# The order of small and big experts in a mixture-of-experts layer

## The chip, the cores and the metric

The kernel runs on one core of a Trainium2 chip. The metric is the device time of one execution in microseconds (us). TensorE does the matrix products, VectorE, ScalarE and GpSimd the elementwise work, SyncE (SP) issues nearly all transfers from device memory (HBM) into the on-chip memory. Each engine runs its own list of instructions in order; semaphores make one wait for another.

## The reference, cut to what matters

A two-layer transformer on 256 tokens of width 1,024, all in 32-bit floats: latent attention and a dense feed-forward layer, then a sparse attention and a mixture-of-experts layer (MoE). The change touches the MoE layer alone. There each token picks two of eight experts, and each expert has three matrices of 1,024 by 3,584 numbers:

```python
logits = (xt @ w_router)                     # 256 x 8
top_val, top_idx = lax.top_k(logits, 2)
wts = softmax(top_val)
for each expert e, on the tokens that picked it:
    h = silu(xb @ w_gate[e]) * (xb @ w_up[e])
    y[tokens] += (h @ w_down[e]) * weight
x = layer_norm(alpha * x + y)
```

The order in which the experts are taken does not enter the result, except through the rounding of the sum. An expert's matrices are 3 x 14 MB = 42 MB (1 MB is 1,024 KB in this text), all eight 336 MB, and each byte is read once.

## The kernel before, in words

**Positions.** The experts are worked off at eight positions. Position 0 is always expert 0, because its loads start before the router has decided. The others are put in order at run time: `arrange` ranks the experts by how many tokens picked them (rank 0 is expert 0, rank 1 the fullest of the rest, rank 7 the emptiest), and the constant `turn` says which rank stands at which position. SP reads the resulting expert numbers into registers and takes the addresses of its loads from them.

**Small and big.** A position in `PLAIN` (called small here) has 64 token slots. Its products take the 32-bit weights as they were loaded, as TensorE's moving operand, with the 64 slots in two halves of the array, and so need no preparation. A position outside `PLAIN` (big) has 128 slots. There each loaded half chunk is split into a rounded part and the rest (`split_half`: ScalarE copies into `whi`, VectorE subtracts into `wlo`), and each product is made of three (high by high, high by low, low by high). The splits go into a ring of half chunks `whi1` to `whi4` and `wlo1` to `wlo4`, so two whole chunks can be split ahead of TensorE. If more tokens picked an expert than it has slots (`most`), an extra pass runs at the end under a condition.

**Chunks and places.** Weights come in chunks of 1 MB, or 768 KB where a step is 1,536 columns wide. An expert has two steps (2,048 and 1,536 hidden columns; position 0 has three: 512, 2,048 and 1,024). For each step `run` does the gate products, half of the down products of the step before, the up products, the other half of the down products. The down products of an expert's last step thus fall between the gate and up products of the next expert. The loads follow this order exactly (`moe_keys`), one list of 364 chunks; position 1 starts with chunk 38, position 2 with chunk 82, position 7 with chunk 312.

Each chunk gets a place by `seq`, which always takes the place used longest ago. There are five raw buffers, seven tiles of 1 MB that are idle in this layer (`xTh`, `xTl`, `xna`, `lng`, `s2`, `x3Tl`, and `x3Th` from chunk 46 on), and the ring's five pairs `R0` to `R4`. The pairs `R1` to `R4` serve as places only up to the chunk in `until`, since the splits need them then; `R0` stays a place. After that there are 13 places, 12 once `lng` has been given back for the final norm's gain (at chunk 312). SP issues the loads in order; a load waits until its place is free: for a small expert when TensorE has used the chunk, for a big one when VectorE has made its `wlo`. A load that waits holds up all loads behind it.

**Order of the work.** TensorE's, VectorE's and ScalarE's order is written out by hand. `pump` splits the next half chunk after each chunk of products, at most five chunks ahead in the list. The MoE layer's first loads are issued from 381 us on, its first small products start at about 502 us.

The functions that the change touches and their surroundings:

Of the kernel before, what the change touches and what calls it, by code (L numbers as in the profile page):

```python
# [20 lines left out]
E = 8  # L21
FE = 3584
FF = 2816
PLAIN = 0, 1, 3, 5, 7


def body(tc, a, out, tap=None, upto=9):
# [31 lines left out]
    HL, NR = 5, 5  # L59
# [292 lines left out]
    if len(cols) % 2:  # L352
        c = plan[-1]
# [15 lines left out]
    def is_plain(key):  # L369

        return key[1] in PLAIN and key[:3] != ("mg", 0, 0)

# [29 lines left out]
    def moe_keys():  # L402
        prev = None
        for e in range(E):
            for j, (c0, wd) in enumerate(widths(e)):
                m = widths(prev[0])[prev[1]][1] // 256 if prev else 0
                for k, ds in (("mg", range((m + 1) // 2)), ("mu", range((m + 1) // 2, m))):
                    yield from ((k, e, j, i) for i in range(n_gu(wd)))
                    yield from (("md", *prev, i) for i in ds)
                prev = e, j  # L410
        yield from (("md", *prev, i) for i in range(wd // 256 - 2))
        yield from (("md", *prev, i, "tail") for i in range(2))
# [5 lines left out]
    keys = list(moe_keys())  # L418

    def seq():  # L420

        at = {f"raw{i}": n for i, n in enumerate((2, 3, 5, 6, 7))}
        at.update({z: first.index(z) for z in ("xTh", "xTl", "xna", "lng", "s2", "x3Tl")})
        at.update({i: first.index(R[i]) for i in range(HL)})

        at["x3Th"] = keys.index(("md", 0, 2, 0))

        until = dict.fromkeys(range(1, HL), keys.index(("mg", 2, 0, 0)) - 8)

        until["lng"] = keys.index(("mg", E - 1, 0, 0))  # L430
        yield from first
        n = len(first)
        while True:
            z = min((z for z in at if n < until.get(z, 9999)), key=at.get)
            at[z] = n
            n += 1
            yield R[z] if z in range(HL) else "raw" if z[:3] == "raw" else z

    seq = [z for _, z in zip(range(len(keys) + 2), seq())]
    for n, key in enumerate(keys):  # L440
        where = seq[n]
# [15 lines left out]
    tie, turn, most = off["tie"], off["turn"], off["most"]  # L457
# [1047 lines left out]
    def gather(e, base, gen=False):  # L1505

        G = {"plain": e in PLAIN and not gen}

# [348 lines left out]
    with tc.If(over > 0):  # L1857
        for e in range(E):
            count = nc.values_load(ordi[0:1, e:e + 1], min_val=0, max_val=256)
            for base in (64, 192) if e in PLAIN else (128,):  # L1860
                with tc.If(count > base):
# [19 lines left out]
def constants():  # L1881
    import numpy as np
    c = {}
    i = np.arange(128)
    c["ident"] = np.eye(128)
    c["tri"] = np.concatenate([np.zeros((128, 128)), np.where(i[None, :] > i[:, None], NEG, 0.0)], 1)
    c["utri"] = (i[:, None] < i[None, :]).astype(np.float64)
    c["iota"] = np.tile(np.arange(320.0), (128, 1))
    e = np.arange(8)
    c["jlt"] = np.tile((e[None, :] < e[:, None]).astype(np.float64).reshape(1, 64), (128, 1))  # L1890
    n = np.arange(16)
    cm = [((128 * t + i[:, None]) >= 16 * n[None, :] + 31) & (n[None, :] < 15) for t in range(2)]
    c["cmask"] = np.concatenate(cm, 1)
    freq = np.power(np.float32(10000.0), -np.arange(32, dtype=np.float32) / np.float32(32))
    ang = np.arange(256, dtype=np.float32)[:, None] * freq[None, :]
    lay = lambda z: np.concatenate([z[:128], z[128:]], 1)
    c["cos"], c["sin"] = lay(np.cos(ang)), lay(np.sin(ang))
    c["nsin"] = -c["sin"]
    c["tie"] = np.tile(np.where(e == 0, 1e6, -e.astype(np.float64)), (128, 1))
    c["turn"] = np.tile(np.array([0.0, 7, 1, 6, 2, 5, 3, 4]), (128, 1))  # L1900
    c["most"] = np.tile(np.where(np.isin(e, PLAIN), 64.0, 128.0), (128, 1))
    packed = np.concatenate([c[k].astype(np.float32) for k, _ in CONST_COLS], 1)
    assert packed.shape[1] == sum(n for _, n in CONST_COLS)
    idx = np.arange(384)
    dist = 255 - idx
    nn = np.maximum(dist, 0)
    nf = np.maximum(nn, 1).astype(np.float32)
    large = 16 + (np.log(nf / np.float32(16)) / np.float32(math.log(8.0)) * np.float32(16)).astype(np.int32)
    bk = np.where(nn < 16, nn, np.minimum(large, 31))
    oh = np.zeros((33, 384), np.float32)  # L1910
    oh[np.where(dist < 0, 32, bk), 383 - idx] = 1.0
    return {"consts": np.ascontiguousarray(packed), "bucket": oh}
# [26 lines left out]
```

## Time and profile before

| what | us |
|---|---|
| median of 3 runs (1328.12 to 1332.17) | 1328.43 |
| the profiled execution | 1331.11 |
| its span, first to last instruction | 1329.3 |

Shares of the span: TensorE 97%, its weight loads 69%, VectorE 54%, ScalarE 45%, GpSimd 2%; the transfers moved 429.52 MB (here millions of bytes), on average 323 GB/s over the span. The profiled execution is 1.8 us longer than its span, and 2.7 us over the median. A TensorE that is busy in the page is not TensorE at its peak, and a wait of it inside a group of products can hide in the busy time, so stretches are compared here by their length, and the loads by when they land.

### The profile page before, as it was taken

Reading aid. Unit: us, or ns where it says so; the run is one execution under the profiler, and the core shown is the slowest. Engines: PE = TensorE matmul, PEld = TensorE weight load, DVE = VectorE, ACT = ScalarE, POOL = GpSimd, SP = SyncE. Lnnn points to the kernel's source line nnn. Section 1 sums busy time; section 2 is a strip of 40 time slices with the busy share of each in tenths; the row PEclk is TensorE's granted clock in tenths of the full one; section 3 lists DMA queues with packets and bytes.
Section 4 is the critical chain, followed back from the end, with each engine's and each line's share of the span. In section 5 each row is a group of like instructions: output and inputs, shape, how many; then the busy total and the mean of one; then the engine's idle time right before and its main releaser. Section 6 shows DMA issues by size and latency. Waiting matters only on the chain.

```text
span 1329.3 us, 19696 instructions
## 1 busy us (share of the span) xinstructions
PE 1293.7 (97%) x7391; PEld 922.4 (69%) x7391; DVE 719.6 (54%) x1206; ACT 594.6 (45%) x948; POOL 29.3 (2%) x52
## 2 busy tenths in 40 slices
PE   8999999999999999999999999999999999999994
PEld 7878999989988673433477955466984557895441
DVE  5757545567778760002278753167963247874313
ACT  5544444455477521100266742056753136673201
POOL 0001000002100000000000000000000000000000
PEclk9999999999999999999999999999999999999998
DMA  9635555579622399999999999999999999999993
GB/s 308 224 96 192 165 186 191 190 196 261 192 79 82 126 359 400 416 418 413 420 420 417 419 419 419 417 420 419 417 419 415 417 420 419 418 407 397 379 409 145
DMA packets 129577, 429.52 MB, mean 323 GB/s; under 512 B 12680, under 2 KB 65174, under 8 KB 103233
## 3 DMA queue, kind: packets, MB, share of 16 engines
q1 hardware_dynamic: 127120, 421.03, 81.8%
q0 software_dynamic: 2352, 7.14, 1.8%
q8 instruction: 60, 0.98, 0.3%
q14 instruction: 45, 0.36, 0.1%
HBM read 427.07 MB, written 1.07 MB: 322 GB/s over the span
## 4 chain that ended last, share of the span: by engine, by line
PE 85%; DMA 8%; DVE 4%; ACT 2%; issue 0%; POOL 0%; SPq 0%; DVEq 0%; ACTq 0%; POOLq 0%
PE pa L1622 32%; PE pb L1622 16%; PE pa L267 6%; PE pa L269 5%; PE pa L268 5%; DMA raw<-in_moe_w_up_dram 3%; DMA raw<-in_moe_w_gate_dram 3%; PE pt L1530 2%; PE pb L267 2%; PE pb L268 2%; PE pb L269 2%; PE pt L1554 1%; PE pb L1236 1%; DMA wlo<-in_moe_w_gate_dram 1%; PE pt L267 1%; DVE wlo L131 1%
## 5 line engine op out<-in xcount | busy, mean ns | idle before, releaser
L131 DVE TENSOR_TENSOR wlo<-raw,whi 128x1024 fp32r<-128x1024 f32 (+3 forms) x371 | 418.5, 1147 | 245.0 <-ACT whi L128 237.8
L128 ACT CAST whi<-raw 128x1024 fp32r<-128x1024 f32 (+3 forms) x371 | 361.9, 989 | 266.5 <-PE pa L1622 70.4
L1622 PE MATMUL pa<-whi,xe 128*128 128x512 f32 (+3 forms) x860 | 251.3, 393 | 1.9 <-ACT whi L128 1.7
L1622 PE MATMUL pa<-raw,xe 128*64 128x512 f32 (+2 forms) x1064 | 223.6, 562 | 0.0
L1622 PEld LDWEIGHTS pa<-whi,xe 128*128 128x128 f32 (+1 forms) x860 | 149.3, 183 | 37.9 <-issue 12.9
L1622 PE MATMUL pa<-wlo,xe 128*128 128x512 f32 (+3 forms) x476 | 163.9, 407 | 0.8 <-DVE wlo L131 0.8
L1622 PEld LDWEIGHTS pa<-raw,xe 128*64 128x64 f32 x1064 | 72.4, 134 | 125.9 <-issue 115.0
L1622 PE MATMUL pb<-whi,four 128*128 128x512 f32 (+1 forms) x376 | 126.9, 418 | 0.0
L1622 PE MATMUL pb<-raw,four 128*64 128x512 f32 x480 | 108.0, 594 | 0.3 <-DMA raw<-in_moe_w_down_dram 0.3
L1760 DVE TENSOR_TENSOR hh<-hh,pa 128x512 f32<-128x512 f32 (+2 forms) x44 | 25.4, 616 | 138.6 <-PE pa L1622 130.1
L1622 PEld LDWEIGHTS pa<-wlo,xe 128*128 128x128 f32 (+1 forms) x476 | 79.1, 178 | 22.0 <-issue 11.0
L1622 PEld LDWEIGHTS pb<-whi,four 128*128 128x128 f32 (+1 forms) x376 | 68.6, 183 | 27.7 <-issue 11.0
L1622 PE MATMUL pb<-wlo,four 128*128 128x512 f32 (+1 forms) x208 | 85.0, 434 | 0.0
L1622 PEld LDWEIGHTS pb<-raw,four 128*64 128x64 f32 x480 | 34.2, 136 | 66.0 <-issue 63.4
L267 PE MATMUL pa<-xTh,whi 128*128 128x256 f32 x216 | 67.5, 313 | 0.0
L269 PE MATMUL pa<-xTh,wlo 128*128 128x256 f32 x216 | 61.1, 283 | 0.5 <-DVE wlo L131 0.5
L268 PE MATMUL pa<-xTl,whi 128*128 128x256 f32 x216 | 61.0, 283 | 0.0
L1747 ACT ACTIVATE hh<-pa 128x512 f32<-128x512 f32 (+2 forms) x44 | 21.9, 543 | 74.9 <-PE pa L1622 74.9
L267 PE MATMUL pb<-xTh,whi 128*128 128x256 f32 x176 | 49.9, 284 | 0.0
L268 PE MATMUL pb<-xTl,whi 128*128 128x256 f32 x176 | 49.8, 283 | 0.0
L269 PE MATMUL pb<-xTh,wlo 128*128 128x256 f32 x176 | 49.8, 283 | 0.0
L1622 PEld LDWEIGHTS pb<-wlo,four 128*128 128x128 f32 (+1 forms) x208 | 37.0, 178 | 10.7 <-issue 3.3
(411 smaller groups left out, 1896.7 us busy)
## 6 DMA issues: line engine op xcount, KB each, us to landing
raw<-in_moe_w_down_dram SPq DMA_DIRECT2D x94, 1024.0 KB, 14.9
raw<-in_moe_w_up_dram SPq DMA_DIRECT2D x60, 1024.0 KB, 13.0
raw<-in_moe_w_gate_dram SPq DMA_DIRECT2D x60, 1024.0 KB, 14.8
raw<-in_moe_w_up_dram SPq DMA_DIRECT2D x52, 768.0 KB, 13.5
raw<-in_moe_w_gate_dram SPq DMA_DIRECT2D x51, 768.0 KB, 15.0
raw<-in_nsa_w_in_dram SPq DMA_DIRECT2D x23, 512.0 KB, 7.2
raw<-in_ffn_w_gate_dram SPq DMA_DIRECT2D x11, 1024.0 KB, 5.4
raw<-in_ffn_w_up_dram SPq DMA_DIRECT2D x11, 1024.0 KB, 5.3
```

Of the source, the lines that this page charges most:

```text
L128: act.copy(hi[:, :h], src)
L131: (pool if later == "pool" else dve).tensor_tensor(lo[:, :h], src, f(hi[:, :h]), op=ALU.subtract)
L267: pe.matmul(o, lh, rh, start=first, stop=False)
L268: pe.matmul(o, lh, rl, start=False, stop=False)
L269: pe.matmul(o, ll, rh, start=False, stop=last)
L1236: pe.matmul(p[:, :2 * nk].rearrange("p (b n) -> p b n", b=2), qT[:, i, t * 128:(t + 1) * 128], kswT[:, g, :, :nk], start=True, stop=True)
L1530: pe.matmul(p[:, i * m:i * m + m], x3[:, t, k * 128:(k + 1) * 128], f(G["oh"][:, t, :m]), start=t == 0, stop=t == 1)
L1554: pe.transpose(p[:, (c - c0) * 128:(c - c0 + 1) * 128], hh[:, c * 128:c * 128 + 128] if plain else hh[:, o:o + 255:2], ident)
L1622: pe.matmul(o, l, r, start=first, stop=last, skip_group_check=True)
L1747: act.activation(z, p, AF.Silu)
L1760: dve.tensor_tensor(z, z, p, op=ALU.mult)
```

## The change

The small and big experts change places, so that the order is small, big, small, big, small, big, small, small; before it was small, small, big, small, big, small, big, small. Three lines hold what follows from that: the set of small positions, the rank at each position, and the chunk from which the ring pairs `R1` to `R4` are no longer places (8 chunks before the first big expert's first one: chunk 30, before it was chunk 74). The ranks stay small or big as they were: ranks 1, 2 and 3 are big, the others small. `most` follows from `PLAIN`.

```diff
-PLAIN = 0, 1, 3, 5, 7
+PLAIN = 0, 2, 4, 6, 7
...
-        until = dict.fromkeys(range(1, HL), keys.index(("mg", 2, 0, 0)) - 8)
+        until = dict.fromkeys(range(1, HL), keys.index(("mg", 1, 0, 0)) - 8)
...
-    c["turn"] = np.tile(np.array([0.0, 7, 1, 6, 2, 5, 3, 4]), (128, 1))
+    c["turn"] = np.tile(np.array([0.0, 1, 7, 2, 6, 3, 5, 4]), (128, 1))
```

## Rows read from the trace of the kernel before

**Rows 1.** The page: TensorE's line of part 1, the GB/s line of part 2.
```profile
PE 1293.7 (97%) x7391; PEld 922.4 (69%) x7391; DVE 719.6 (54%) x1206; ACT 594.6 (45%) x948; POOL 29.3 (2%) x52
...
GB/s 308 224 96 192 165 186 191 190 196 261 192 79 82 126 359 400 416 418 413 420 420 417 419 419 419 417 420 419 417 419 415 417 420 419 418 407 397 379 409 145
```
**Rows 2.** Windows of positions 2 to 7: length, PE, PEld, DVE, ACT, POOL, clock, DMA, GB/s.
```profile
655.00:779.95 124.95, 122.56 (x594) 99.83 (x596) 98.92 (x103) 84.38 (x98) 0.00 (x0) 0.99 1.02 419
779.95:872.39 92.44, 92.44 (x455) 43.18 (x455) 28.92 (x34) 23.09 (x29) 0.00 (x0) 1.00 1.02 419
872.39:992.63 120.24, 120.24 (x594) 98.66 (x596) 94.74 (x98) 80.38 (x94) 0.00 (x0) 1.00 1.02 419
992.63:1085.14 92.51, 92.51 (x456) 43.22 (x455) 29.84 (x34) 23.10 (x29) 0.00 (x0) 1.00 1.02 417
1085.14:1205.47 120.33, 120.33 (x595) 98.63 (x596) 93.90 (x97) 80.53 (x94) 0.00 (x0) 1.00 1.01 415
1205.47:1310.60 105.13, 105.00 (x493) 46.10 (x494) 25.55 (x31) 20.87 (x28) 0.00 (x0) 1.00 0.95 374
```
**Rows 3.** Chain of waits, pieces: start, length, line, products (pa: gate, up; pb: down).
```profile
548.05 6.87 PE pb L1622 x32
...
573.66 1.80 PE pa L1622 x8
...
796.65 8.56 PE pb L1622 x36
...
872.39 2.99 PE pa L1622 x12
...
1309.54 1.01 PE pb L1622 x4
```
**Rows 4.** Timeline of PE at position 2's start: start, length, products, idle time before.
```profile
656.22 0.50 PE L1622 MATMUL pa<-whi,xe 128*128 128x512 f32 x1 [1.67 <-ACT whi L128]
657.48 0.71 PE L1622 MATMUL pa<-wlo,xe 128*128 128x512 f32 x1 [0.76 <-DVE wlo L131]
```
**Rows 5.** The window of these waits, columns as in rows 2.
```profile
655.00:662.00 7.00, 5.02 (x15) 3.76 (x16) 5.80 (x7) 5.14 (x6) 0.00 (x0) 0.76 1.01 419
```
**Rows 6.** SP's timeline, each issue followed by its DMA row, last number: us to landing.
```profile
448.65 0.34 SPq L91 DMA_DIRECT2D raw<-in_moe_w_gate_dram  x1
raw<-in_moe_w_gate_dram SPq DMA_DIRECT2D x1, 1024.0 KB, 5.1
...
541.50 0.35 SPq L91 DMA_DIRECT2D raw<-in_moe_w_gate_dram  x1
raw<-in_moe_w_gate_dram SPq DMA_DIRECT2D x1, 1024.0 KB, 13.0
...
638.95 0.33 SPq L91 DMA_DIRECT2D raw<-in_moe_w_gate_dram  x1
raw<-in_moe_w_gate_dram SPq DMA_DIRECT2D x1, 1024.0 KB, 16.1
...
787.68 0.33 SPq L91 DMA_DIRECT2D raw<-in_moe_w_up_dram  x1
raw<-in_moe_w_up_dram SPq DMA_DIRECT2D x1, 1024.0 KB, 11.3
...
849.94 0.33 SPq L91 DMA_DIRECT2D raw<-in_moe_w_gate_dram  x1
raw<-in_moe_w_gate_dram SPq DMA_DIRECT2D x1, 1024.0 KB, 16.6
...
997.73 0.33 SPq L91 DMA_DIRECT2D raw<-in_moe_w_up_dram  x1
raw<-in_moe_w_up_dram SPq DMA_DIRECT2D x1, 1024.0 KB, 10.2
...
1292.02 1.82 SPq L82 DMA_DIRECT2D raw<-in_moe_w_down_dram  x2
raw<-in_moe_w_down_dram SPq DMA_DIRECT2D x1, 512.0 KB, 13.9
```

## The prediction

> **What bounds the kernel now.** I read the page first: TensorE is busy 97% of the span, and from the 15th slice on the transfers move 400 to 420 GB/s in nearly every slice [rows 1]. Two resources look full at once, so neither share says which one ends the kernel. The windows, cut where the first gate product of an expert starts, separate them [rows 2]. A window of a small expert after a big one takes 92.44 us, a window of a big expert after a small one 120.24 us, and both move about 418 GB/s. So the loads run at one pace all the time, while TensorE is alternately faster and slower than they are. What lies between them is the set of places into which chunks are loaded. An expert is 42 MB here (1 MB for 1,024 KB); the first chunk of position 2 is issued at 638.95 and lands 16.1 later, at 655.05, that of position 4 at 849.94 + 16.6 = 866.5 [rows 6]. That is 211.5 us for 84 MB, 2.517 us per MB, against 92.44 + 120.24 = 212.7 of TensorE work [rows 2]. The pair is balanced to 1.2 us.
>
> I call **lead** the time from a chunk's landing to its first product, and **lag** the time from its issue to its landing. A shrinking lead ends in a TensorE wait. A shrinking lag means that SP issues late because no place is free, and ends in idle transfers. Before the change the two small experts at positions 0 and 1 use up the lead: position 1 starts at 573.66 [rows 3] with its first chunk landed at 541.50 + 13.0 = 554.5 [rows 6], a lead of 19.2. At the end of it TensorE waits for the split of the first big chunk (1.67 and 0.76 us idle [rows 4], granted clock 0.76 in those 7 us [rows 5]): the window of position 2 takes 124.95 instead of 120.24 [rows 2]. That is the only loss on TensorE's side; after it TensorE is full up to the end.
>
> **The change part by part.** *The work itself* is the same: five small and three big experts, the same products, loads, splits and gathers, in another order. The constants only hold other numbers. One edge differs: position 0's last step is 1,024 wide, with 4 down chunks instead of 6, and they now fall into a big window. A small expert's down chunk costs 6.87 / 4 = 1.72, a big one's 8.56 / 3 = 2.85 [rows 3].
>
> *The wait at position 2 goes.* A big expert at position 1 finds 19.2 us of lead, so nothing there waits for a landing; the split keeps up too, with VectorE busy 94.74 of the 120.24 us [rows 2]. TensorE's own schedule would be: 573.66 + (120.24 - 2 x 1.72 = 116.8) + 92.44 + 120.24 + 92.51 + 120.33 + 92.44 = 1208.4 for the start of position 7, and for that position 105.13 - 6 x (2.85 - 1.72) = 98.3, since the down chunks before it are now small: 1306.8 [rows 2, 3]. Before, the last window ends at 1310.60. By TensorE alone the change gains 3.8 us.
>
> *What is late next: the places.* In a big window the transfers gain on TensorE. How far may they? Lead at a big expert's start and smallest lag behind it: position 2 would start, unwaited, at 779.95 - 120.24 = 659.7, lead 659.7 - 655.05 = 4.65, and the smallest lag, near the turn to position 3, is 11.3 (issue at 787.68); position 4 has 872.39 - 866.5 = 5.9 and then 10.2 (issue at 997.73) [rows 2, 3, 6]. The sums are 15.95 and 16.1: with 13 places lead and smallest lag share 16.0 us. Now position 1 is the big one, with a lead of 19.2, and its window leaves 116.8 for TensorE against 40 x 2.517 = 100.7 of loads, 16.1 gained where a later window gains 120.24 - 105.7 = 14.5: 1.6 more. The lag would have to be 16.0 - 19.2 - 1.6 = -4.8. A chunk that is alone takes 5.1 [rows 6], so I put the floor at 5.1, and the transfers stand idle for 4.8 + 5.1 = 9.9 us between about 600 and 720. After that the lead at position 3 is 16.0 - 5.1 + 1.2 = 12.1, the lag behind it 3.9, 1.2 under the floor; the same behind position 5. Together 9.9 + 2 x 1.2 = 12.3 us of idle transfers. Bounds: the nearest thing to no floor is the chunk's own 2.5 us, which gives 7.3 + 2.4 = 9.7; if a shallow queue costs 3 us more each time, 21. I take 12.3, since the lone chunk is the row closest to a queue that has run dry. The Trainium skill ("DMA: Bandwidth & Descriptors", Anatomy of one DMA) puts a transfer at 2.0 us plus its bytes at 436 GB/s, given there for the software queue; for 1 MB that is an estimate of 4.4, and the sum would be 0.7 less; this case's lone chunk has 5.1.
>
> *What the transfers get back.* From 866.5 to the last landing, 1293.3 + 13.9 = 1307.2 (the second issue of the pair at 1292.02 [rows 6]), 173 MB take 440.7 where 2.517 per MB makes 435.4: they lost 5.2 in the last third, behind position 6, where the lead had grown so far that SP found no free place. In the new order the last big expert is position 5, and positions 6 and 7 are both small: this loss goes.
>
> *The earlier end of the four ring places* (load 30 instead of 74) leaves 12 places at position 1's first loads. The chunk issued at 541.50 would wait for the first down chunk of step 1, consumed at 548.05 + 1.72 = 549.8 [rows 3], and its lag falls from 13.0 to 4.7. That is at the floor, so I cost it at nothing; whatever is lost there (bounds 0 to 2) is lost out of the same 9.9, not beside it, because a later landing leaves less lead to give away.
>
> **The sum.** Last landing 1307.2 - 5.2 + 12.3 = 1314.3, 7.1 later. TensorE's 1306.8 lies ahead of that by 7.5, so it waits for loads in position 7: lead 12 at its start, 47 x 2.517 = 118 of loads against 98 of work. The end hangs on the last landing as it does now (22.1 us from it to the span's end). Span 1329.3 + 7.1 = 1336.4, that execution 1331.11 + 7.1 = 1338.2; it lay 2.7 over the median of the runs, 1328.43, and against that I predict 1335.5.
>
> **Rivals.**
> *The places hold the first big expert.* If the smallest lag near 700 to 720 stays above 5, nothing idles there; with the 5.2 gone the last landing would be near 1302 and TensorE's 1306.8 decides: 3.8 us faster, 1324.6. It speaks for it that the loads now run only at 419 with 13 places; against it the sum of 16.0, met twice. It decides as soon as the lag has over 10 us more room than I give it. 0.09.
> *Half of it.* The floor is 2.5 and the extra 1.6 is not there: 5.7 + 2.4 - 5.2 = 2.9 us, 1331.3, within what a measurement tells apart (0.3%, 4 us). For it: single lags under 5 could occur in a queue that is never quite empty. 0.16.
> *The clock falls in position 7.* There TensorE would idle some 0.75 us per chunk of 2.5 us. After the idle times of 1.67 and 0.76 us at 655 the granted clock was 0.76 over 7 us, so in part at 1.2 GHz [rows 4, 5]. If it stayed at that level, a small chunk would take 3.44, more than its 2.5 of loading, over the last 17 MB or so: 16 us more, 1352. Against it: at 3.44 per chunk TensorE would be full again, and over the whole window of position 2 the clock was 0.99 [rows 2]. 0.08. The Trainium skill ("TensorE: Matmul & The Clock Gate", Loop structure matters more than you think) has the same rule, that a loop which waits for a transfer ahead of its products runs cold; the trace here shows it for the one gap only.
> *Shallow queues cost more.* Three stretches run at the floor instead of one; at 2 to 3 us more each, 1341 to 1344. 0.10.
> *It doesn't do what it says*: the three fullest experts behind position 0 stay the big ones and the thresholds move with them, so no extra pass can start that did not start before. I see no way; it gets no chance.
>
> **How the numbers follow.** The forecast has 0.57. Slower by over 0.3%: 0.57 + 0.08 + 0.10 = 0.75; within 0.3% 0.16; faster 0.09. The range goes from the half case with 3 us of room, 1328, to the shallow-queue case, 1345, and leaves out most of the faster one and of the clock.
>
> **What would show it.** Right: no TensorE wait near 655; GB/s under 400 in slices between 600 and 720; lags of about 5 at the turn from position 1 to 2; small dips near 910 and 1120; none near 1240; TensorE waiting for raw chunks in the last third of position 7; a last landing near 1314. Wrong: a full GB/s row at 600 to 720 (the first rival), or TensorE full up to the end with a span above 1333 (then some work was longer, and not the places).

## The result, and the profile after

The changed kernel takes 1337.57 us (median of 5 runs, 1337.08 to 1338.47) against 1330.13 for the kernel before beside it: the ratio is 1.0057, 95% interval 1.0045 to 1.0070, so it is slower, by 7.4 us. The profiled execution took 1338.47, its span is 1336.6 (before: 1331.11 and 1329.3). Landings are compared between profiled executions, which do not all reach the experts at the same moment: TensorE starts position 1 at 573.66 before [rows 3], at 574.03 in this one, and between 571.3 and 575.0 in the runs further down; where that matters, the difference is given. The prediction had 7.1 us more, 1335.5, and a span of 1336.4.

The page of the changed kernel, the row that answers to [rows 1]; a slice is 33.4 us:

```profile
GB/s 320 210 95 191 173 176 189 189 195 275 190 66 94 127 373 397 385 419 387 371 368 416 418 420 418 417 418 395 417 421 420 416 419 393 417 419 420 418 419 184
```

The row has dips where before it was flat: slices 19 to 21 (602 to 702 us) at 387, 371 and 368, slice 28 (from 902) at 395, slice 34 (from 1103) at 393. Before, the dip lay behind position 6, in slices 36 to 39 [rows 1]; there the row is now full up to the last slice.

Windows of the changed kernel, cut at the first gate product of positions 1 to 7, and the last part of position 7, columns as in [rows 2]:

```profile
574.03:690.66 116.63, 116.63 (x576) 97.25 (x578) 93.51 (x96) 80.83 (x94) 0.00 (x0) 1.00 0.99 389
690.66:783.30 92.64, 92.64 (x456) 42.81 (x455) 29.84 (x34) 23.11 (x29) 0.00 (x0) 1.00 1.01 409
783.30:903.66 120.36, 120.36 (x595) 98.57 (x596) 94.13 (x97) 80.84 (x94) 0.00 (x0) 1.00 1.02 418
903.66:996.29 92.63, 92.63 (x456) 42.76 (x455) 29.83 (x34) 23.02 (x29) 0.00 (x0) 1.00 1.01 410
996.29:1116.58 120.29, 120.29 (x594) 98.63 (x596) 94.12 (x97) 80.84 (x94) 0.00 (x0) 1.00 1.02 418
1116.58:1208.96 92.38, 92.38 (x457) 43.32 (x458) 23.92 (x28) 18.59 (x25) 0.00 (x0) 1.00 1.01 409
1208.96:1317.70 108.74, 99.87 (x461) 33.77 (x458) 8.92 (x14) 8.04 (x14) 0.00 (x0) 1.00 1.00 409
...
1255.00:1317.00 62.00, 53.13 (x253) 17.60 (x251) 5.88 (x10) 2.74 (x5) 0.00 (x0) 1.00 1.00 406
```

The windows of TensorE have the lengths that the kernel before leads one to expect: 92.4 to 92.6 for a small expert behind a big one and 120.3 for a big one, as there, and 116.63 for the first big expert, whose window holds two down chunks fewer (the prediction had 116.8). Nothing of the work got longer, and from position 1 to position 7 TensorE does not wait. Only the last window has idle time, 108.74 - 99.87 = 8.9 us.

Two views say what that idle time waits for. First TensorE's timeline near the end (start, length, products, in brackets the idle time before and its releaser), then the chain of waits of the same stretch:

```profile
1290.10 1.57 PE L1622 MATMUL pa<-raw,xe 128*64 128x384 f32 x8 [0.31 <-DMA raw<-in_moe_w_up_dram]
...
1299.46 1.94 PE L1622 MATMUL pb<-raw,four 128*64 128x512 f32 x8 [0.28 <-DMA raw<-in_moe_w_down_dram]
1301.94 1.94 PE L1622 MATMUL pb<-raw,four 128*64 128x512 f32 x8 [0.54 <-DMA raw<-in_moe_w_down_dram]
1304.52 1.94 PE L1622 MATMUL pb<-raw,four 128*64 128x512 f32 x8 [0.65 <-DMA raw<-in_moe_w_down_dram]
1306.95 1.94 PE L1622 MATMUL pb<-raw,four 128*64 128x512 f32 x8 [0.49 <-DMA raw<-in_moe_w_down_dram]
```

```profile
1255.62 13.72 DMA raw<-in_moe_w_down_dram
...
1269.46 14.95 DMA raw<-in_moe_w_up_dram
...
1284.53 17.36 DMA raw<-in_moe_w_down_dram
...
1302.01 13.91 DMA raw<-in_moe_w_down_dram
...
1317.70 1.01 PE pb L1622 x4
```

TensorE takes each chunk as it lands, one per 2.5 us, and from 1255 on the chain is made of loads. Before, the chain at this place was TensorE's own work from end to end (its longest piece below), and its last product [rows 3] ended 3.35 us after the last landing, since it still had chunks in hand.

```profile
1293.74 13.91 PE pb L1622 x64
```

Where the loads lost their time is read from SP's timeline, each issue followed by its row of the transfers (last number: us from issue to landing), as in [rows 6]. The rows are the first chunk of position 1, one late in position 1, the first of position 2, one of its up products, and the last pair:

```profile
548.34 0.35 SPq L91 DMA_DIRECT2D raw<-in_moe_w_gate_dram  x1
raw<-in_moe_w_gate_dram SPq DMA_DIRECT2D x1, 1024.0 KB, 8.2
...
643.15 0.33 SPq L91 DMA_DIRECT2D raw<-in_moe_w_up_dram  x1
raw<-in_moe_w_up_dram SPq DMA_DIRECT2D x1, 768.0 KB, 4.5
...
655.84 0.33 SPq L91 DMA_DIRECT2D raw<-in_moe_w_gate_dram  x1
raw<-in_moe_w_gate_dram SPq DMA_DIRECT2D x1, 1024.0 KB, 7.1
...
695.77 0.33 SPq L91 DMA_DIRECT2D raw<-in_moe_w_up_dram  x1
raw<-in_moe_w_up_dram SPq DMA_DIRECT2D x1, 1024.0 KB, 7.3
...
1302.01 3.33 SPq L82 DMA_DIRECT2D raw<-in_moe_w_down_dram  x2
raw<-in_moe_w_down_dram SPq DMA_DIRECT2D x2, 512.0 KB, 13.3
```

The lags of 13.0 and 16.1 us of the first chunks of positions 1 and 2 [rows 6] have become 8.2 and 7.1: SP issues the load only when the transfers have nearly run dry. What it waited for, position 1 and the start of position 2 (waits of SP's queue: total us, times, longest):

```profile
SPq L91 <- DVE wlo L131: 68.6, 30, 3.6
SPq L91 <- PE pb L1622: 12.0, 5, 4.6
SPq L91 <- PE pa L1622: 8.3, 3, 3.7
```

30 of these waits are for a `wlo`: for the split of a chunk of the big expert, which frees its place. It can be no more than two chunks ahead of TensorE, and so these loads go at TensorE's pace.

The landings of the first chunk of each position, after minus before, add up the loss (us, from the same two columns of both traces):

| first chunk of position | 1 | 2 | 3 | 4 | 5 | 6 | 7 | last chunk |
|---|---|---|---|---|---|---|---|---|
| lands later by | 2.0 | 7.9 | 11.4 | 12.4 | 13.8 | 13.8 | 15.0 | 10.0 |

0.4 of it is there before position 1 starts (574.03 against 573.66 [rows 3]).

### The profile page after: what moved, and what is told of

It is laid out like the page before. It is cut to its first block, busy times and chain, and to the rows that moved or that the text cites. A ratio compares the mean times of both kernels' runs of the same rounds, so it can differ in the third digit from the quotient of the medians.

```text
span 1336.6 us, 19668 instructions
## 1 busy us (share of the span) xinstructions
PE 1296.0 (97%) x7391; PEld 919.5 (69%) x7391; DVE 720.6 (54%) x1206; ACT 595.8 (45%) x948; POOL 29.3 (2%) x52
## 4 chain that ended last, share of the span: by engine, by line
PE 89%; DMA 5%; DVE 4%; ACT 1%; issue 0%; POOL 0%; SPq 0%; DVEq 0%; ACTq 0%; POOLq 0%
PE pa L1622 35%; PE pb L1622 16%; PE pa L267 6%; PE pa L268 5%; PE pa L269 5%; DMA raw<-in_moe_w_down_dram 3%; PE pt L1530 2%; PE pb L267 2%; PE pb L268 2%; PE pb L269 2%; PE pt L1554 1%; PE pb L1236 1%; PE pt L267 1%; PE pt L269 1%; PE pt L268 1%; DMA raw<-in_moe_w_up_dram 1%
## 5 line engine op out<-in xcount | busy, mean ns | idle before, releaser
L131 DVE TENSOR_TENSOR wlo<-raw,whi 128x1024 fp32r<-128x1024 f32 (+3 forms) x359 | 407.1, 1152 | 209.9 <-ACT whi L128 203.6
L128 ACT CAST whi<-raw 128x1024 fp32r<-128x1024 f32 (+3 forms) x359 | 352.9, 994 | 231.5 <-PE pa L1622 70.2
L1622 PE MATMUL pa<-raw,xe 128*64 128x512 f32 (+2 forms) x1144 | 239.9, 564 | 2.5 <-DMA raw<-in_moe_w_up_dram 2.5
L1622 PE MATMUL pa<-whi,xe 128*128 128x512 f32 (+3 forms) x820 | 240.5, 383 | 0.0
L1622 PEld LDWEIGHTS pa<-raw,xe 128*64 128x64 f32 x1144 | 76.8, 134 | 140.7 <-issue 123.6
L1622 PE MATMUL pa<-wlo,xe 128*128 128x384 f32 (+3 forms) x436 | 153.4, 390 | 0.0
L1622 PE MATMUL pb<-raw,four 128*64 128x512 f32 x528 | 120.3, 596 | 6.4 <-DMA raw<-in_moe_w_down_dram 6.4
L1622 PE MATMUL pb<-whi,four 128*128 128x512 f32 (+1 forms) x352 | 115.4, 406 | 0.0
L1622 PE MATMUL pb<-wlo,four 128*128 128x512 f32 (+1 forms) x184 | 74.0, 414 | 0.0
L1560 ACT COPY four<-pt 128x512 f32<-128x512 f32 (+1 forms) x11 | 6.2, 564 | 91.5 <-PE pt L1554 91.5
```

The lines of the kernel that those rows point to most:

```text
L128: act.copy(hi[:, :h], src)
L131: (pool if later == "pool" else dve).tensor_tensor(lo[:, :h], src, f(hi[:, :h]), op=ALU.subtract)
L1560: (dve.tensor_copy if c0 else act.copy)(z, p[:, :n * 128])
L1622: pe.matmul(o, l, r, start=first, stop=last, skip_group_check=True)
```

## The experiments

Theory (places): the end is set by the loads, and they lost their time because the first big expert now meets a full lead, more than the 13 places can hold. Rivals: the work of TensorE got longer; it is the two small experts in a row at the end; it is the line on the ring's places; idle transfers count wherever they are. All ratios are against the kernel before on the same chip; for the changed kernel that is 1.0057.

**What ends the kernel: more work for TensorE at position 7.** In both kernels:

```diff
                         mm(o[64 * q:64 * q + 64], x[:, k, 0:64], z[:, q::2], k == 0, k == 7)
+                if (which, e, j) == ("mg", E - 1, 0) and i in (1, 2, 3, 4):
+                    o = pT()
+                    for z in raw_of(*key):
+                        for q in range(2):
+                            mm(o[64 * q:64 * q + 64], x[:, i, 0:64], z[:, q::2], True, True)
```

> The changed kernel with 16 extra products on four gate chunks of position 7 (their result is thrown away), about 4 x 1.8 = 7.2 us more for TensorE. Theory (places: the last position now waits for its loads): TensorE has about 10 us to spare there, so the time stays within 1.5 us of the changed kernel, about 1338, last landing within 1 us of its 1317.2. Rival (the changed kernel ends by TensorE's work, and some of that got longer): 7 us more, about 1345.

> The kernel before with the same 16 extra products at position 7. Theory (before, TensorE's work ends the kernel, the loads are just done): 5.5 to 7.2 us slower than before, about 1336. Rival (before, the loads end it too): about 1.5 us slower, the time TensorE lags behind the last landing being the only one lost.

Measured: the changed kernel with the extra work 1336.08, ratio 1.0045 (1.0030 to 1.0061), no slower than without it; the kernel before with it 1335.58 against 1329.89, ratio 1.0053 (1.0035 to 1.0070), 7.0 us by the ratio, 5.7 by the medians. TensorE's waits for loads in position 7 of the changed kernel (total us, times, longest), first without, then with the extra products:

```profile
PE pb L1622 <- DMA raw<-in_moe_w_down_dram: 6.4, 11, 1.0
PE pa L1622 <- DMA raw<-in_moe_w_up_dram: 2.5, 6, 0.9
```

```profile
PE pb L1622 <- DMA raw<-in_moe_w_down_dram: 3.6, 6, 1.0
PE pa L1622 <- DMA raw<-in_moe_w_up_dram: 0.6, 2, 0.3
```

The waits shrink from 8.9 to 4.2 us: the work went into them. (The last landing is 1.4 us later than the 1317.2 of the changed kernel, where at most 1 was expected; 0.5 of it is there when position 1 starts.) So the kernel before ends by TensorE, the changed one by its loads. "Longer work" is out.

**Fewer places.** In the changed kernel:

```diff
+        until["s2"] = until["x3Tl"] = until[1]
         until["lng"] = keys.index(("mg", E - 1, 0, 0))
```

> The changed kernel with two places fewer (s2 and x3Tl are no longer places from chunk 30 on). Theory (transfers stand idle at the first big expert because no place is free): lead and smallest lag share 2 chunks less, so 2 x 2.5 to 2 x 2.8 us more idle at the turn from position 1 to 2 and nothing more at the later turns: 5.0 to 5.6 us slower than the changed kernel, about 1343. Rival (the loss comes from the order at the end, two small experts in a row, and not from the places): no change, 1337.6.

Measured: 1341.41, ratio 1.0088 (1.0064 to 1.0113), 4 us above the changed kernel by the ratios, but the two intervals touch, so the time alone would leave it open. The trace shows more. Below are the first chunk of position 3 and TensorE's first product of position 1 in this run, and then that product in the changed kernel:

```profile
762.85 0.33 SPq L91 DMA_DIRECT2D raw<-in_moe_w_gate_dram  x1
raw<-in_moe_w_gate_dram SPq DMA_DIRECT2D x1, 1024.0 KB, 13.1
```

```profile
571.25 0.50 PE L1623 MATMUL pa<-whi,xe 128*128 128x512 f32 x1
```

```profile
573.96 0.50 PE L1622 MATMUL pa<-whi,xe 128*128 128x512 f32 x1
```

The chunk lands at 762.85 + 13.1 = 775.95, 2.8 later than in the changed kernel (773.1). But this execution reached position 1 2.7 us earlier; ahead of the experts, from 484 to 492 us, its granted clock was 1.00, and in the execution of the changed kernel 0.79. Counted from the start of position 1, the chunk lands 5.5 us later, inside the 5.0 to 5.6 of the theory. The last chunk lands 1.7 later, 4.4 counted in the same way: about 1 us comes back at the later turns, which the expectation left out. So the places set what is lost at the turn, and by the size forecast.

**The first big expert early, the end as before.** In the changed kernel:

```diff
-PLAIN = 0, 2, 4, 6, 7
+PLAIN = 0, 2, 3, 5, 7
...
-    c["turn"] = np.tile(np.array([0.0, 1, 7, 2, 6, 3, 5, 4]), (128, 1))
+    c["turn"] = np.tile(np.array([0.0, 1, 7, 6, 2, 5, 3, 4]), (128, 1))
```

> Order small, big, small, small, big, small, big, small: the first big expert at position 1 as in the changed kernel, the last four positions as in the kernel before. Theory (places): the transfers lose about 11 us at the turn from position 1 to 2, the two small experts then use the lead up, TensorE waits at the start of position 4 (chunk 174 lands near 878), and ends TensorE-bound 8 to 10 us after the kernel before, about 1339. Rival (two small experts in a row at the end are what costs): as the kernel before, 1330.

Measured: 1340.78, ratio 1.0075 (1.0053 to 1.0096), 10 us slower than before by the ratio. The last four positions are those of before, and it is as slow as the changed kernel or slower: two small experts at the end are not what costs. SP's timeline for the first chunk of position 4, and TensorE's at its start:

```profile
863.71 0.33 SPq L91 DMA_DIRECT2D raw<-in_moe_w_gate_dram  x1
raw<-in_moe_w_gate_dram SPq DMA_DIRECT2D x1, 1024.0 KB, 16.1
```

```profile
877.41 1.94 PE L1622 MATMUL pb<-raw,four 128*64 128x512 f32 x8 [0.54 <-DMA raw<-in_moe_w_down_dram]
880.97 0.50 PE L1622 MATMUL pa<-whi,xe 128*128 128x512 f32 x1 [1.62 <-ACT whi L128]
882.24 0.50 PE L1622 MATMUL pa<-wlo,xe 128*128 128x512 f32 x1 [0.76 <-DVE wlo L131]
```

The chunk lands at 879.8 where about 878 was expected, and TensorE pays the lost transfers here, at the next place where the lead runs out, instead of at the end.

**Two big experts in a row, the start as before.** In the kernel before, `PLAIN = 0, 1, 3, 6, 7` and ranks 0, 7, 1, 6, 2, 3, 5, 4 (the order is small, small, big, small, big, big, small, small):

> Order small, small, big, small, big, big, small, small: positions 0 to 4 as in the kernel before, two big experts in a row at 4 and 5. Theory (places): no idle transfers up to position 4, then at the turn from 5 to 6 the lead would have to be 5.9 + 14.5 + 21.3 (127 us of work against 105.7 of loads), so about 16 us of idle transfers there; last landing 1307.2 - 5.2 + 16 = 1318, about 8 us slower than before, 1338. Rival (the loss belongs to the start, where the four ring places end early): as before, 1330.

Measured: 1343.81, ratio 1.0100 (1.0084 to 1.0115), 13 us slower by the ratio, where 8 were expected. The row of the page:

```profile
GB/s 314 214 95 190 181 172 185 187 196 284 192 67 77 142 382 400 417 416 414 420 420 417 419 420 416 419 420 417 417 420 358 310 363 374 419 418 421 418 418 170
```

Full up to slice 30, then 358, 310, 363 and 374 from about 1007 to 1141 us, where the second of the two big experts and the turn behind it are. So the same loss can be put anywhere: it sits where a big expert meets a lead that is already long. The size was underestimated: the first chunk of position 7 lands at 1191.11 + 13.4 = 1204.5, 20.0 later than before (1184.5), and the last one 15.1 later (1322.3 against 1307.2). Of the 20.0, 0.8 is there before the second big expert starts (its first chunk lands at 958.14 + 15.8 = 973.9, before at 973.1), so 19.2 us were lost where about 16 were expected.

**The line on the ring's places alone.** In the kernel before, `("mg", 2, 0, 0)` becomes `("mg", 1, 0, 0)`:

> The kernel before with only the one line on the ring's places changed (they end as places at chunk 30 instead of 74, unused in between). Theory (places): the first loads of position 1 are issued later, 1.5 to 2 us of transfers are lost, and TensorE waits that much longer at the start of position 2: 1 to 3 us slower than before. Rival (this line is what costs in the changed kernel): about 7 us slower, 1337.

Measured: 1329.75 against 1328.88, ratio 1.0000 (0.9991 to 1.0009). The time is the same within 1.2 us, where 1 to 3 were expected. TensorE does wait a little more: from the start of position 1 to that of position 2 it takes 82.64 us (571.61 to 654.25) against 80.90 before, and its last product is 1.0 later counted from there. As the cause of the 7 us in the changed kernel, this line is out.

**The lead that is lost anyway.** In the kernel before (with the line just tried) and in the changed kernel, four places are left out for chunks 24 to 45:

```diff
+        pause = dict.fromkeys(("xna", "lng", "s2", "x3Tl"), at["x3Th"])
...
-            z = min((z for z in at if n < until.get(z, 9999)), key=at.get)
+            z = min((z for z in at if pause.get(z, 0) <= n < until.get(z, 9999)), key=at.get)
```

> The kernel before, with the ring's places ended at chunk 30 (which alone cost nothing) and four more places (xna, lng, s2, x3Tl) paused for chunks 24 to 45, so that loads of position 0 and 1 find 8 places instead of 12 and the transfers stand idle there for about 7 to 10 us. Theory (before, positions 0 and 1 use up the lead, so each us of it counts): TensorE waits that much longer towards the start of position 2, 7 to 10 us slower than before, about 1338. Rival (early lead is worth nothing in either order): as before, 1329.

> The changed kernel with the same four places paused for chunks 24 to 45: the transfers stand idle for some 6 to 8 us more during position 0. Theory (the first big expert's window finds no place for the lead it is given, so the lead is lost there anyway): what is lost early is not lost again at the turn from position 1 to 2; within 2 us of the changed kernel, 1337 to 1339, and chunk 128 lands within 2 us of its 773.1. Rival (idle transfers simply add up, whatever their place): 6 to 8 us slower than the changed kernel, about 1344.

Measured: the kernel before 1339.94, ratio 1.0071 (1.0050 to 1.0093), about 9.5 us slower by the ratio; the changed kernel 1337.06, ratio 1.0052 (1.0035 to 1.0069), no slower than without the pause. Windows of position 0, of most of position 1, and of the turn to position 2 (last number: GB/s): the changed kernel without the pause, then with it:

```profile
500.00:574.00 74.00, 73.06 (x370) 27.98 (x369) 9.49 (x13) 12.30 (x18) 0.00 (x0) 1.00 0.99 394
574.00:640.00 66.00, 66.00 (x308) 51.31 (x307) 52.98 (x55) 45.02 (x51) 0.00 (x0) 1.00 1.00 404
640.00:725.00 85.00, 85.00 (x424) 61.33 (x424) 54.31 (x56) 48.54 (x59) 0.00 (x0) 1.00 0.98 379
```

```profile
500.00:574.00 74.00, 73.06 (x366) 27.78 (x365) 9.58 (x13) 12.49 (x18) 0.00 (x0) 1.00 0.86 339
574.00:640.00 66.00, 66.00 (x309) 51.44 (x308) 53.85 (x56) 45.68 (x52) 0.00 (x0) 1.00 1.02 419
640.00:725.00 85.00, 85.00 (x422) 60.81 (x422) 53.42 (x54) 47.86 (x58) 0.00 (x0) 1.00 1.01 414
```

With the pause the transfers move 339 instead of 394 GB/s during position 0, and 419 and 414 instead of 404 and 379 after it. The first chunk of position 1 lands at 556.14 + 9.1 = 565.2, 8.7 later than without the pause, that of position 3 at 759.91 + 13.4 = 773.3, 0.2 later than 773.1. (This execution starts position 1 0.9 us earlier than the one without the pause, so from there it is 1.1.) The changed kernel gives away the lead that the loads have at position 1; the kernel before lives on it. That is the theory's mechanism, with the sum left unchanged by moving the idle time.

## Why the prediction was right, point by point

| step | predicted | measured |
|---|---|---|
| TensorE at position 2 / at position 7, without waits | 690.5 / 1208.4 | 690.66 / 1208.96 |
| wait at position 2 gone | yes | no wait from position 1 to 6 |
| idle transfers, turn from 1 to 2, with what is lost before it | 9.9 | 11.4 - 0.4 = 11.0 |
| the same behind positions 3 and 5 | 1.2 + 1.2 | 2.4 + 1.2 |
| transfers get back in position 7 | 5.2 | 15.0 - 10.0 = 5.0 |
| last landing | 7.1 later, 1314.3 | 10.0 later, 1317.2 |
| from there to the span's end | 22.1 | 19.4 |
| span, difference of the medians | 1336.4, 7.1 | 1336.6, 7.4 |

The mechanism, its place and its sign are shown by the runs above: loads end the changed kernel (extra work is free there, and not before), they are late because of the first big expert (the orders and the pause) and of the number of places (two fewer, 5.5 us at the turn), and the one line costs at most 1.2 us.

The total is closer than its terms, and that is luck: two of them were off in opposite directions. *What a low lag costs* was too low. I let the transfers stand idle only when the lag is at the 5.1 of a chunk that is alone, and then took 9.9 + 1.2 + 1.2. The smallest lags of 1 MB chunks behind positions 1, 3 and 5 are 5.9, 5.4 and 5.0, so the floor was near, but the transfers lose time before they reach it: in the rows above the chunks with a lag of 7.1 and 7.3 land 2.8 and 3.7 us after the one before them, where 2.5 is the pace. The idle times were 11.0, 2.4 and 1.2, together 2.3 us more; the bounds that I gave reached to 21. With 0.4 from before position 1 and 0.2 less got back in position 7, the last landing is 2.9 later than forecast. The two big experts in a row show the same, 19.2 against about 16. *The end* was too long: I said that it hangs on the last landing with the same 22.1 us, though by my own sum TensorE would then be waiting and no longer behind. Its last product ends 1317.70 + 1.01 - 1317.2 = 1.5 after the last landing instead of 3.35, which is 1.8 of the 2.7. The other 0.9 lies behind the last product, a stretch that takes between 17.1 and 18.9 us in the ten traces, and does not follow the edits (two variants of the kernel before have 17.1, the kernel before has 18.8), so I count it as chance. The two errors, 2.9 and 2.7, cancel.

*The early end of the ring places* was costed at nothing, and by the time it is nothing within 1.2 us. The sentence that what is lost early is lost out of the same sum is what the pause shows most clearly: 8.7 us lost before position 1 came back to within about 1, and the time did not grow.

*The rivals.* The places did not hold the first big expert. The half case is out by over 4 us. The clock did not fall: in the last 62 us TensorE waits 8.9 us, at most 1.0 at a time, and the granted clock of that window is 1.00, 2.4 GHz throughout. For the rule of the Trainium skill ("TensorE: Matmul & The Clock Gate", Loop structure matters more than you think), that a loop with a long wait for a transfer ahead of its products runs cold, this trace is no example: these waits are short. The one drop of [rows 5] followed a 1.67 us wait. Shallow queues do cost more than the floor of 5.1 says, as the fourth rival had it, but about 1 us at two of the three turns and not 2 to 3 at each.

No run here beats the kernel before. By the same sum, the most that this order could gain is an estimated 3.8 us, TensorE's own schedule, and it would need the lead of position 1 and places for 7 to 10 us more of loads at the same time; no run here has more places.

## What to carry to other kernels

Where two resources are balanced on average, an order of the work is worth what the buffer between them can hold: follow the lead (landing to use) and the lag (issue to landing) through the stages, because a stage in which the transfers gain is wasted when it meets a full buffer, however balanced the whole is. Read the room from two rows of the trace, lead at the start of such a stage and smallest lag behind it. Their sum was 15.95 and 16.1 us in two stages with 13 places and carried the forecast; the third big expert before, at position 6, whose loads behind it find 12 places, has 7.2 + 6.1 = 13.3 (first chunk landed at 1062.70 + 15.3 = 1078.0, issue at 1213.19), about one chunk's 2.5 us less. And compare landings of two executions from a common point of the work, or a few us of early difference pass for an effect. An early idle transfer need not cost anything, nor an extra piece of work: ask which of the two the end waits for first.

## What was not expected of the hardware

The queue of transfers loses pace before it is empty. A chunk of 1 MB alone takes 5.1 us [rows 6], but in the changed kernel between 640 and 705 us lags of 6 to 7.3 us often went with landings of 1 MB chunks 2.8 to 3.8 us apart instead of 2.5, and the same is seen in both variants with other orders. It is no fixed lag at which this begins: near 1120 two chunks in a row with lags of 5.6 and 5.0 land at 1124.2 and 1126.7, still 2.5 apart. What decides it stays open.

```profile
1118.58 0.33 SPq L91 DMA_DIRECT2D raw<-in_moe_w_up_dram  x1
raw<-in_moe_w_up_dram SPq DMA_DIRECT2D x1, 1024.0 KB, 5.6
...
1121.68 0.33 SPq L91 DMA_DIRECT2D raw<-in_moe_w_up_dram  x1
raw<-in_moe_w_up_dram SPq DMA_DIRECT2D x1, 1024.0 KB, 5.0
```

TensorE's granted clock stayed at 2.4 GHz through 17 waits of at most 1.0 us for single chunks. Nor does the pair of waits before the drop of [rows 5] always bring one: in the run with the line on the ring's places alone, waits of 1.6 and 0.8 us at the start of position 2 left the granted clock at 1.00, and the position (below) took 124.87 us, against 125.39 cut in the same way in the kernel before, where it fell, and 120.24 for a big expert without these waits. So nearly all of that loss is the wait's and not the clock's.

```profile
654.25:779.12 124.87, 120.92 (x595) 98.62 (x596) 98.72 (x103) 84.33 (x98) 0.00 (x0) 1.00 1.02 419
```
